# Softmax attention in a two-layer decoder trunk: weights normalised by GpSimd and streamed against values held in column halves

## The chip, the cores and the metric

One core of a Trainium2 chip runs the whole program. The metric is device time in microseconds (us). Engines are called by the letters of the profile: PE (TensorE, the matmul array), PEld (its weight loads), DVE (VectorE), ACT (ScalarE), POOL (GpSimd), SP (SyncE, which issues the weight loads from HBM).

## The reference

Two layers, each a half-weighted SwiGLU FFN, a token mixing and a second such FFN, then a final RMS norm; 256 tokens, width 1024, all in float32. The mixing projects the normalised tokens once (`w_in`) and splits the result over three groups that share the output projection: six retention heads of 64, six attention heads of 64, and a 31-tap causal depthwise convolution over 256 channels. The attention is MoBA, but 256 tokens are a single block of its 256, so it comes down to causal softmax attention over all keys:

```python
s_own = jnp.einsum('bhqd,bhkd->bhqk', qblk, k_own).astype(jnp.float32) * scale
causal = (own * bs + klocal)[None, :] <= qpos[:, None]
s_list = [jnp.where(causal, s_own, -jnp.inf)]
...
p = jax.nn.softmax(jnp.concatenate(s_list, -1), axis=-1).astype(v.dtype)
out = jnp.einsum('bhqk,bhkd->bhqd', p[..., :bs], v_own)
```

## The kernel before

Every large product is a loop over weights that stream from HBM. A weight piece (`raw`) is cut into two parts of reduced precision, `whi` by ACT (L147) and `wlo` by DVE (L148), and each product is three matmuls, L203 to L205. After a piece has been used the loop calls `tick()`. The small work of the mixing (attention, retention, convolution, rotation) is written as generators, the chains: a chain issues some instructions, then says `yield n` to wait n ticks (or until a named mark is done), so its PE instructions stand between the projection's pieces. The order of PE's instructions is the order of the program; on DVE, ACT and POOL a scheduler puts the instructions in an order at build time, and each engine then works through its list in that order.

The attention chain `moba(t)` handles 128 queries (t is 0 or 1). It spawns a `moba_group` for a few heads at a time: three pairs of heads for t = 0, which sees 128 keys, and two pairs, then one, for t = 1, which sees 256. Of each pair the even head goes to one half-group (j = 0) and the odd one to the other (j = 1). In a group, PE writes the mask and the scores to two PSUM banks (L725, L729); DVE takes the maximum of each row (L733); ACT takes the exponentials into the SBUF tile `pr` and the row sums into `sums` (L740). After four ticks PE transposes the weights (L747), ACT copies them to SBUF (L749, `hf`), and PE multiplies them with the values (L759): the weights, 128 x 128, are loaded as the stationary operand and the 64 columns of one head's values are streamed. The result in the bank `po` has queries as partitions. When all groups are through, DVE takes the reciprocal of the sums (L771) and multiplies `po` by it on its way to SBUF (L773); `into_mix` transposes the three 128-column blocks on PE (L781) and `split` cuts them in two parts (ACT L198, DVE L199) into `mT`, the input of the output projection.

Other work that the prediction speaks of: the convolution's taps, 62 instructions on DVE in each layer (L866: two tensors in SBUF, `u` and the running sum `ac`); the rotation of the retention's queries and keys, of which DVE makes two products from PSUM (L699, L700) and POOL the sum of two SBUF tiles of 128 x 384 (L701), four times in each layer; the retention's scores on PE (L794), multiplied by the decay on DVE (L801), which frees the scores' PSUM banks for the next group, and then multiplied with the values (L809); and POOL's multiplications by a broadcast factor in the norm of the retention (L827, 384 columns) and of the convolution (L888, 512 columns), whose factors POOL makes as powers (L476, and L495 elsewhere).

Of the kernel before, what the change touches and what calls it, by code (L numbers as in the profile page):

```python
# [11 lines left out]
F32 = mybir.dt.float32  # L12
# [3 lines left out]
AF = mybir.ActivationFunctionType  # L16
OP = mybir.AluOpType
# [5 lines left out]
P = 128  # L23
# [5 lines left out]
H = 6  # L29
HD = 64  # L30
HW = H * HD
# [24 lines left out]
class Kernel:  # L56
# [166 lines left out]
    def setup(self):  # L223
        nc, c, a = self.nc, self.const, self.a
        self.mhalf = c.tile([P, 8], F32, tag="mhalf", name="mhalf")
        nc.gpsimd.memset(self.mhalf, -0.5)
        warm = c.tile([P, 8], F32, tag="warm", name="warm")
        nc.scalar.activation(warm, self.mhalf, AF.Silu)
        self.x = [c.tile([P, D], F32, tag=f"x{t}", name=f"x{t}") for t in range(NT)]
        for t in range(NT):  # L230
            for h in range(2):
                n = slice(h * 512, (h + 1) * 512)
                nc.sync.dma_start(self.x[t][:, n], a["x"][t][:, n])
        self.row = self.act.tile([P, D + 8], F32, tag="g", bufs=1, name="row")[0:1, :D]
        nc.scalar.dma_start(self.row, a["fgain"][0:1])
        self.ident = self.load("ident", (P, P), eng=nc.scalar)
# [419 lines left out]
    def mix(self, l, cur, nxt):  # L656
        nc, a = self.nc, self.a
        hT = cur.hT
        mT = self.new_hT()
        with self.tc.tile_pool(name=f"mix{l}", bufs=1) as mp:  # L660

            def tl(tag, shape, bufs=1):
                return mp.tile(shape, F32, tag=tag, bufs=bufs, name=self.name(tag))

            def chunk(w, t, free):
                ps = self.mmb()
                self.projA(ps, t, hT, w, HW, free)
                return ps[:, :HW]

            def heads(x):  # L670
                return x.rearrange("p (h d) -> p h d", h=H)
# [34 lines left out]
            def values(tag, ps):  # L706
                v = tl(tag, [P, HW], 2)
                nc.scalar.activation(v, ps, AF.Copy)
                return v

            def groups(t):
                return [(0, 3)] if t == 0 else [(0, 2), (4, 1)]

            def hs(x, h, lo, hi):
                b = (h % 2) * HD
                return x[b:b + HD, h // 2, lo:hi]

            def moba_group(t, g0, nh, po, sums):
                nk = t + 1
                n = nk * P  # L720
                nb = nh * nk
                banks = [self.acc()[:, :nb * P].rearrange("p (h k) -> p h k", h=nh) for _ in range(2)]
                mask = self.mask16[:, 2 * P - n:][:, None, :].to_broadcast([P, nh, n])
                for sc in banks:
                    nc.tensor.matmul(sc, self.ident16, mask, start=True, stop=False)  # L725
                for i in range(nh):
                    for j, sc in enumerate(banks):
                        h = g0 + 2 * i + j
                        nc.tensor.matmul(sc[:, i], hs(mqT, h, t * P, (t + 1) * P), hs(mkT, h, 0, n), start=False, stop=i == nh - 1)  # L729
                nms, prs = [], []  # L730
                for sc in banks:
                    nm = self.small.tile([P, 4], F32, tag="nm", name=self.name("nm"))
                    nc.vector.tensor_reduce(nm[:, :nh], sc, axis=AX.X, op=OP.max, negate=True)  # L733
                    nms.append(nm)
                for j, sc in enumerate(banks):
                    pr = self.scratch()
                    pv = pr[:, :nb * P].rearrange("p (h k) -> p h k", h=nh)
                    for i in range(nh):
                        h = g0 + 2 * i + j
                        nc.scalar.activation(pv[:, i], sc[:, i], AF.Exp, bias=nms[j][:, i:i + 1], accum_out=sums[:, h:h + 1])  # L740
                    prs.append(pr)
                yield 4
                sts = []
                for j in range(2):
                    pt = self.trb()
                    for i in range(nb):
                        nc.tensor.transpose(pt[:, i * P:(i + 1) * P], prs[j][:, i * P:(i + 1) * P], self.ident)  # L747
                    st = self.scratch()
                    nc.scalar.activation(st[:, :nb * P], pt[:, :nb * P], AF.Copy)  # L749
                    sts.append(st)  # L750
                    yield 1
                yield 1
                for j in range(2):
                    for i in range(nh):
                        h = g0 + 2 * i + j
                        for kb in range(nk):
                            c = (i * nk + kb) * P
                            hd = slice(h * HD, (h + 1) * HD)
                            nc.tensor.matmul(po[:, hd], sts[j][:, c:c + P], mv[kb][:, hd], start=kb == 0, stop=kb == nk - 1)  # L759
                self.done.add(f"mg{t}{g0}{l}")  # L760

            def moba(t):
                yield self.has(*[f"{x}{i}{l}" for x in ("mq", "mk") for i in range(t + 1)])
                po = self.acc()
                sums = self.small.tile([P, 8], F32, tag="sm", name=self.name("sm"))
                for h0, nh in groups(t):
                    self.spawn(moba_group(t, h0, nh, po, sums))
                    yield 2
                yield self.has(*[f"mg{t}{h0}{l}" for h0, _ in groups(t)])
                rc = self.small.tile([P, 8], F32, tag="rc", name=self.name("rc"))  # L770
                nc.vector.reciprocal(rc[:, :H], sums[:, :H])  # L771
                yn = tl("w", [P, HW], 5)
                nc.vector.tensor_tensor(heads(yn), heads(po[:, :HW]), rc[:, :H, None].to_broadcast([P, H, HD]), op=OP.mult)  # L773
                yield 2
                into_mix(yn, 3, t)
                self.done.add(f"moba{t}{l}")

            def into_mix(yn, k0, t):
                ps = self.trb()
                for j in range(3):  # L780
                    nc.tensor.transpose(ps[:, j * P:(j + 1) * P], yn[:, j * P:(j + 1) * P], self.ident)  # L781
                sl = (slice(None), slice(k0, k0 + 3), slice(t * P, (t + 1) * P))
                self.split(mT[0][sl], mT[1][sl], ps[:, :HW].rearrange("p (k s) -> p k s", k=3))
# [135 lines left out]
            w = self.take(4)  # L919
            mv = [values("mv", chunk(w, 0, False))]  # L920
            self.spawn(moba(0))
            mv.append(values("mv", chunk(w, 1, True)))
            self.spawn(moba(1))
            w = self.take(4)
            for t in range(NT):
                self.spawn(rot(chunk(w, t, t == 1), t, rqT, "rq"))
            w = self.take(4)
            for t in range(NT):
                self.spawn(rot(chunk(w, t, t == 1), t, rkT, "rk"))
            w = self.take(4)  # L930
            rv = [values("rv", chunk(w, t, t == 1)) for t in range(NT)]
            w = self.take(4)
# [203 lines left out]
```

## Time and profile before

| what | value |
|---|---|
| median of 3 runs | 991.15 us (990.84 to 991.24) |
| profiled execution | 988.81 us |
| its span | 987.0 us |
| mean granted TensorE clock | 0.998 |
| busy: PE, DVE, ACT, POOL | 976.8, 683.8, 537.1, 67.5 us |

The span is the stretch from the first to the last recorded instruction of the profiled execution; the execution's own time lies 1.8 us above it and 2.3 us below the median. Busy shares are averages: PE is busy 99% of the span and DVE 69%, but in the mixing DVE is far busier than on average. One layer takes 485 us, and the second repeats the first's mixing; rows are shown from the first.

### The profile page before, as it was taken

How to read it: one execution, taken by the hardware profiler on the slowest of the kernel's cores; microseconds unless marked ns; L12 is line 12 of the kernel's file. 1: busy time of each engine (PE TensorE's matmuls, PEld its weight loads, DVE VectorE, ACT ScalarE, POOL GpSimd, SP SyncE). 2: the span in 40 equal slices, each digit the busy share in tenths (PEclk: the TensorE clock that was granted, in tenths of full speed). 3: DMA queues.
4: the chain of work that ended last, by engine and by line, in shares of the span. 5: the costliest groups of instructions: out<-in, count | busy, mean ns of one | idle time of the engine just before them, and what ended most of it. 6: DMA issues, size and time to landing. Idle time of an engine off the chain costs nothing.

```text
span 987.0 us, 13779 instructions
## 1 busy us (share of the span) xinstructions
PE 976.8 (99%) x5321; PEld 850.1 (86%) x5321; DVE 683.8 (69%) x1030; ACT 537.1 (54%) x904; POOL 67.5 (7%) x115
## 2 busy tenths in 40 slices
PE   9999999999999999999999999999999999999997
PEld 6888888898998888888888888888989888888885
DVE  5987565669976866666676656566799677666653
ACT  5755555366554755555465555554665456555542
POOL 0101000021140000000000000002100400000000
PEclk9999999999999999999999999999999999999999
DMA  7975555345542855555546464543545346555511
GB/s 258 334 273 178 205 180 180 119 152 190 171 171 70 309 199 174 208 175 206 176 183 223 171 210 173 205 142 136 193 144 199 135 151 254 176 208 173 209 45 43
DMA packets 28580, 180.17 MB, mean 183 GB/s; under 512 B 3425, under 2 KB 3809, under 8 KB 10338
## 3 DMA queue, kind: packets, MB, share of 16 engines
q1 hardware_dynamic: 27216, 175.54, 51.1%
q10 hardware_dynamic: 1298, 3.74, 1.0%
q8 instruction: 42, 0.69, 0.3%
q14 instruction: 24, 0.20, 0.1%
HBM read 178.22 MB, written 1.05 MB: 182 GB/s over the span
## 4 chain that ended last, share of the span: by engine, by line
PE 92%; DVE 5%; ACT 1%; DMA 1%; issue 1%; POOL 0%; SPq 0%; POOLq 0%; ACTq 0%; DVEq 0%
PE mm L209 15%; PE tr L209 15%; PE acc L614 8%; PE acc L613 8%; PE acc L617 8%; PE tr L210 8%; PE mm L210 8%; PE mm L203 4%; PE mm L205 4%; PE mm L204 4%; DVE wlo L148 2%; DVE ac L866 2%; PE acc L209 1%; PE mm L326 1%; PE tr L505 1%; PE acc L809 1%
## 5 line engine op out<-in xcount | busy, mean ns | idle before, releaser
L148 DVE TENSOR_TENSOR wlo<-raw,whi 128x1024 fp32r<-128x1024 f32 (+1 forms) x340 | 397.9, 1181 | 172.8 <-ACT whi L147 168.9
L147 ACT ACTIVATE whi<-raw 128x1024 fp32r<-128x1024 f32 (+1 forms) x340 | 344.0, 1023 | 213.1 <-PE acc L617 84.7
L209 PE MATMUL mm<-hT,whi 128*128 128x512 f32 x640 | 226.1, 391 | 0.0
L209 PE MATMUL tr<-hT,whi 128*128 128x512 f32 x640 | 225.9, 391 | 0.0
L210 PE MATMUL tr<-hT,wlo 128*128 128x256 f32 x640 | 180.5, 282 | 0.0
L210 PE MATMUL mm<-hT,wlo 128*128 128x256 f32 x640 | 180.4, 282 | 0.0
L209 PEld LDWEIGHTS mm<-hT,whi 128*128 128x128 f32 x640 | 120.1, 188 | 25.9
L209 PEld LDWEIGHTS tr<-hT,whi 128*128 128x128 f32 x640 | 120.1, 188 | 25.1
L613 PE MATMUL acc<-whi,hf 128*128 128x512 f32 x352 | 137.7, 391 | 0.0
L614 PE MATMUL acc<-wlo,hf 128*128 128x512 f32 x352 | 137.2, 390 | 0.0
L210 PEld LDWEIGHTS mm<-hT,wlo 128*128 128x128 f32 x640 | 120.8, 189 | 1.4
L210 PEld LDWEIGHTS tr<-hT,wlo 128*128 128x128 f32 x640 | 121.0, 189 | 0.0
L617 PE MATMUL acc<-whi,hf 128*128 128x512 f32 x352 | 113.6, 389 | 0.0
L203 PE MATMUL mm<-whi,hT 128*128 128x384 f32 (+1 forms) x272 | 99.3, 365 | 0.0
L205 PE MATMUL mm<-whi,hT 128*128 128x384 f32 (+1 forms) x272 | 94.2, 346 | 0.0
L204 PE MATMUL mm<-wlo,hT 128*128 128x384 f32 (+1 forms) x272 | 94.1, 346 | 0.0
L617 PEld LDWEIGHTS acc<-whi,hf 128*128 128x128 f32 x352 | 66.1, 188 | 13.9
L599 ACT ACTIVATE s<-part 128x256 f32<-128x256 f32 x80 | 33.2, 416 | 82.2 <-DVE part L215 82.0
L613 PEld LDWEIGHTS acc<-whi,hf 128*128 128x128 f32 x352 | 66.1, 188 | 13.6
L614 PEld LDWEIGHTS acc<-wlo,hf 128*128 128x128 f32 x352 | 66.2, 188 | 12.3
L215 DVE TENSOR_TENSOR part<-part,tr 128x256 f32<-128x256 f32 x80 | 33.5, 419 | 47.3 <-ACT part L214 47.3
L866 DVE SCALAR_TENSOR_TENSOR ac<-u,vec,ac 128x256 f32<-128x256 f32 x120 | 56.6, 525 | 0.0
(179 smaller groups left out, 983.2 us busy)
## 6 DMA issues: line engine op xcount, KB each, us to landing
raw<-in_wgb SPq DMA_DIRECT2D x80, 1024.0 KB, 4.9
raw<-in_wd SPq DMA_DIRECT2D x44, 1024.0 KB, 4.9
raw<-in_win SPq DMA_DIRECT2D x28, 768.0 KB, 5.1
raw<-in_wout SPq DMA_DIRECT2D x8, 1024.0 KB, 4.9
raw<-in_wga SPq DMA_DIRECT2D x6, 1024.0 KB, 5.4
raw<-in_wcv SPq DMA_DIRECT2D x4, 1024.0 KB, 5.0
raw<-in_wga SPq DMA_DIRECT2D x8, 256.0 KB, 5.6
g<-in_fgain ACTq DMA_DIRECT2D x3, 512.0 KB, 3.9
```

Source lines behind the costliest of these rows:

```text
L147: nc.scalar.activation(hi[:, c], src, AF.Copy)
L148: nc.vector.tensor_tensor(lo[:, c], src, hi[:, c].bitcast(F32), op=OP.subtract)
L203: mm(out, ah, wh, start=start, stop=False)
L204: mm(out, ah, wl, start=False, stop=False)
L205: mm(out, al, wh, start=False, stop=stop)
L209: mm(out, wh, x, start=start, stop=False)
L210: mm(out[:, :S], wl, x[:, 0], start=False, stop=stop)
L215: self.nc.vector.tensor_tensor(v, lo, ps[:, :S], op=OP.add)
L613: mm(ys[t][h], hi[:, ts], wh[:, n], start=first, stop=False)
L614: mm(ys[t][h], hi[:, ts], wl[:, n], start=False, stop=False)
L617: mm(ys[t][h], lo[:, ts], wh[:, n], start=False, stop=last)
L866: nc.vector.scalar_tensor_tensor(ac[ct], us, wj, ac[ct], op0=OP.mult, op1=OP.add)
```

## The change

The row sums are kept in two tiles, one for each half-group. Behind each half-group's exponentials POOL now raises its sums to the power -1 (L745 in the new numbering, against a constant tile `mone`) and multiplies the half-group's weights in place by the result, broadcast along the keys (L746). The wait before the transposes of the weights grows from four ticks to six. In the product with the values the operands are exchanged: a head's values, 128 keys x 64 columns, are the stationary operand, the transposed weights are streamed, and even and odd heads are written by turns to the lower and the upper 64 partitions of `po`, which so holds the result transposed. The reciprocal, the normalising multiplication on DVE and the three transposes behind them are gone, and `split` reads `po`. Lines move by 2 above the attention chain, by 6 in its middle (L747 is now L753, L749 is L755, L759 is L766) and by 3 below it.

```diff
--- before.py
+++ after.py
@@ -224,6 +224,8 @@
         nc, c, a = self.nc, self.const, self.a
         self.mhalf = c.tile([P, 8], F32, tag="mhalf", name="mhalf")
         nc.gpsimd.memset(self.mhalf, -0.5)
+        self.mone = c.tile([P, 64], F32, tag="mone", name="mone")
+        nc.gpsimd.memset(self.mone, -1.0)
         warm = c.tile([P, 8], F32, tag="warm", name="warm")
         nc.scalar.activation(warm, self.mhalf, AF.Silu)
         self.x = [c.tile([P, D], F32, tag=f"x{t}", name=f"x{t}") for t in range(NT)]
@@ -737,9 +739,13 @@
                     pv = pr[:, :nb * P].rearrange("p (h k) -> p h k", h=nh)
                     for i in range(nh):
                         h = g0 + 2 * i + j
-                        nc.scalar.activation(pv[:, i], sc[:, i], AF.Exp, bias=nms[j][:, i:i + 1], accum_out=sums[:, h:h + 1])
+                        nc.scalar.activation(pv[:, i], sc[:, i], AF.Exp, bias=nms[j][:, i:i + 1], accum_out=sums[j][:, h // 2:h // 2 + 1])
+                    r = self.small.tile([P, 4], F32, tag="rc", name=self.name("rc"))
+                    g = g0 // 2
+                    nc.gpsimd.tensor_tensor(r[:, :nh], sums[j][:, g:g + nh], self.mone[:, :nh], op=OP.pow)
+                    nc.gpsimd.tensor_tensor(pv, pv, r[:, :nh, None].to_broadcast([P, nh, n]), op=OP.mult)
                     prs.append(pr)
-                yield 4
+                yield 6
                 sts = []
                 for j in range(2):
                     pt = self.trb()
@@ -750,29 +756,26 @@
                     sts.append(st)
                     yield 1
                 yield 1
-                for j in range(2):
-                    for i in range(nh):
-                        h = g0 + 2 * i + j
-                        for kb in range(nk):
-                            c = (i * nk + kb) * P
-                            hd = slice(h * HD, (h + 1) * HD)
-                            nc.tensor.matmul(po[:, hd], sts[j][:, c:c + P], mv[kb][:, hd], start=kb == 0, stop=kb == nk - 1)
+                for i in range(nh):
+                    pair = g0 // 2 + i
+                    for kb in range(nk):
+                        c = (i * nk + kb) * P
+                        for j in range(2):
+                            hd = slice(pair * P + j * HD, pair * P + (j + 1) * HD)
+                            o = po[j * HD:(j + 1) * HD, pair * P:(pair + 1) * P]
+                            nc.tensor.matmul(o, mv[kb][:, hd], sts[j][:, c:c + P], start=kb == 0, stop=kb == nk - 1)
                 self.done.add(f"mg{t}{g0}{l}")
 
             def moba(t):
                 yield self.has(*[f"{x}{i}{l}" for x in ("mq", "mk") for i in range(t + 1)])
                 po = self.acc()
-                sums = self.small.tile([P, 8], F32, tag="sm", name=self.name("sm"))
+                sums = [self.small.tile([P, 4], F32, tag=f"sm{j}", name=self.name("sm")) for j in range(2)]
                 for h0, nh in groups(t):
                     self.spawn(moba_group(t, h0, nh, po, sums))
                     yield 2
                 yield self.has(*[f"mg{t}{h0}{l}" for h0, _ in groups(t)])
-                rc = self.small.tile([P, 8], F32, tag="rc", name=self.name("rc"))
-                nc.vector.reciprocal(rc[:, :H], sums[:, :H])
-                yn = tl("w", [P, HW], 5)
-                nc.vector.tensor_tensor(heads(yn), heads(po[:, :HW]), rc[:, :H, None].to_broadcast([P, H, HD]), op=OP.mult)
-                yield 2
-                into_mix(yn, 3, t)
+                sl = (slice(None), slice(3, 6), slice(t * P, (t + 1) * P))
+                self.split(mT[0][sl], mT[1][sl], po[:, :HW].rearrange("p (k s) -> p k s", k=3))
                 self.done.add(f"moba{t}{l}")
 
             def into_mix(yn, k0, t):
```

The program's order on three engines, each at one place in the first layer's mixing.

POOL, from the end of the rotation of the attention's keys (`w_2370`) to that of the retention (`w_2583` and on), before:

```order
L687 TENSOR_TENSOR r_513_2372<-w_2370,pc 128x96
L688 TENSOR_TENSOR r_514_2373<-w_2370,pn 128x96
L689 TENSOR_TENSOR w_2370<-r_513_2372,r_514_2373 128x6x16
L701 TENSOR_TENSOR w_2583<-w_2583,w_2584 128x384
L701 TENSOR_TENSOR w_2683<-w_2683,w_2684 128x384
L701 TENSOR_TENSOR w_2734<-w_2734,w_2735 128x384
```

The same place now, from the first half-group's weights (`hf_2453`, t = 0; their power stands just ahead) on; the `sm` tiles hold sums and the `rc` tiles their inverses:

```order
L746 TENSOR_TENSOR hf_2453<-hf_2453,rc_2457 128x384
L745 TENSOR_TENSOR rc_2464<-sm_2438,mone 128x3
L746 TENSOR_TENSOR hf_2460<-hf_2460,rc_2464 128x384
L745 TENSOR_TENSOR rc_2534<-sm_2517,mone 128x2
L746 TENSOR_TENSOR hf_2531<-hf_2531,rc_2534 128x512
L745 TENSOR_TENSOR rc_2540<-sm_2518,mone 128x2
L746 TENSOR_TENSOR hf_2537<-hf_2537,rc_2540 128x512
L745 TENSOR_TENSOR rc_2577<-sm_2517,mone 128x1
L746 TENSOR_TENSOR hf_2575<-hf_2575,rc_2577 128x256
L745 TENSOR_TENSOR rc_2582<-sm_2518,mone 128x1
L746 TENSOR_TENSOR hf_2580<-hf_2580,rc_2582 128x256
L703 TENSOR_TENSOR w_2599<-w_2599,w_2600 128x384
```

With that power twelve instructions have come between the two, and all of them stand ahead of the retention's first sum (now L703).

ACT, where the last weights of t = 1 are made, before (`hf_2545` is the second half of t = 0's transposed weights, `hf_2565` and `hf_2567` are t = 1's last weights):

```order
L708 ACTIVATE mv_2496<-mm_2419 128x384
L749 ACTIVATE hf_2511<-tr_2507 128x384
L740 ACTIVATE hf_2527,sm_2514<-acc_2515,nm_2523 128x256 x2
L740 ACTIVATE hf_2530,sm_2514<-acc_2516,nm_2525 128x256 x2
L749 ACTIVATE hf_2545<-tr_2541 128x384
L740 ACTIVATE hf_2565,sm_2514<-acc_2555,nm_2561 128x256
L740 ACTIVATE hf_2567,sm_2514<-acc_2556,nm_2563 128x256
L147 ACTIVATE whi_2597<-raw_2426 128x768
```

And now, where t = 0's second half is `hf_2597`, and t = 1's last weights are `hf_2575` and `hf_2580`:

```order
L710 ACTIVATE mv_2505<-mm_2421 128x384
L742 ACTIVATE hf_2531,sm_2517<-acc_2519,nm_2527 128x256 x2
L742 ACTIVATE hf_2537,sm_2518<-acc_2520,nm_2529 128x256 x2
L755 ACTIVATE hf_2563<-tr_2559 128x384
L742 ACTIVATE hf_2575,sm_2517<-acc_2565,nm_2571 128x256
L742 ACTIVATE hf_2580,sm_2518<-acc_2566,nm_2573 128x256
L755 ACTIVATE hf_2597<-tr_2593 128x384
L147 ACTIVATE whi_2613<-raw_2428 128x768
```

The copy of t = 0's second half has moved behind t = 1's last exponentials.

DVE, around the retention's decays, before (`hf_2904` and `hf_2906` are t = 0's, `hf_2919` and `hf_2921` t = 1's first):

```order
L866 SCALAR_TENSOR_TENSOR ac_436_2027<-u_2025,vec,ac_436_2027 128x256
L866 SCALAR_TENSOR_TENSOR ac_437_2028<-u_2025,vec,ac_437_2028 128x256
L148 TENSOR_TENSOR wlo_2846<-raw_2746,whi_2845 128x1024
L148 TENSOR_TENSOR wlo_2856<-raw_2746,whi_2855 128x1024
L148 TENSOR_TENSOR wlo_2873<-raw_2783,whi_2872 128x1024
L148 TENSOR_TENSOR wlo_2883<-raw_2783,whi_2882 128x1024
L801 TENSOR_TENSOR hf_2904<-acc_2896,decay 128x384
L801 TENSOR_TENSOR hf_2906<-acc_2897,decay 128x384
L866 SCALAR_TENSOR_TENSOR ac_436_2027<-u_2025,vec,ac_436_2027 128x256
L866 SCALAR_TENSOR_TENSOR ac_437_2028<-u_2025,vec,ac_437_2028 128x256
L801 TENSOR_TENSOR hf_2919<-acc_2909,decay 128x512
L801 TENSOR_TENSOR hf_2921<-acc_2910,decay 128x512
```

And now, where the decays are L804 and the taps L869:

```order
L869 SCALAR_TENSOR_TENSOR ac_436_2029<-u_2027,vec,ac_436_2029 128x256
L148 TENSOR_TENSOR wlo_2852<-raw_2756,whi_2851 128x1024
L148 TENSOR_TENSOR wlo_2862<-raw_2756,whi_2861 128x1024
L869 SCALAR_TENSOR_TENSOR ac_437_2030<-u_2027,vec,ac_437_2030 128x256
L148 TENSOR_TENSOR wlo_2879<-raw_2789,whi_2878 128x1024
L148 TENSOR_TENSOR wlo_2889<-raw_2789,whi_2888 128x1024
L804 TENSOR_TENSOR hf_2910<-acc_2902,decay 128x384
L804 TENSOR_TENSOR hf_2912<-acc_2903,decay 128x384
L869 SCALAR_TENSOR_TENSOR ac_436_2029<-u_2027,vec,ac_436_2029 128x256
L804 TENSOR_TENSOR hf_2925<-acc_2915,decay 128x512
L804 TENSOR_TENSOR hf_2927<-acc_2916,decay 128x512
```

Four instructions of DVE are gone from each layer, but the first decay is only two places nearer to the start of its list (the 332nd instead of the 334th): two more taps stand ahead of it.

## Rows read from the trace of the kernel before

**Rows 1.** The page: each engine's busy time in us, share of the span, instructions

```profile
PE 976.8 (99%) x5321; PEld 850.1 (86%) x5321; DVE 683.8 (69%) x1030; ACT 537.1 (54%) x904; POOL 67.5 (7%) x115
```

**Rows 2.** Windows in the mixing: stretch, length, each engine's busy time (instructions), clock, DMA

```profile
245.00:260.00 15.00, 15.00 (x104) 14.85 (x104) 14.94 (x29) 6.83 (x12) 2.87 (x3) 1.00 0.43 145
260.00:275.00 15.00, 15.00 (x108) 14.53 (x107) 15.00 (x23) 10.79 (x14) 1.48 (x2) 1.00 0.47 149
```

**Rows 3.** Waits of PE's weight loads, 225 to 300 us: total, times, longest

```profile
PEld acc L759 <- ACT hf L749: 0.5, 1, 0.5
...
PEld acc L794 <- DVE hf L801: 0.2, 1, 0.2
```

**Rows 4.** DVE's timeline around the decays: start, time from first to last end

```profile
275.65 1.00 DVE L801 TENSOR_TENSOR hf<-acc,decay 128x384 f32<-128x384 f32 x2
276.59 0.86 DVE L866 SCALAR_TENSOR_TENSOR ac<-u,vec,ac 128x256 f32<-128x256 f32 x2
277.37 1.27 DVE L801 TENSOR_TENSOR hf<-acc,decay 128x512 f32<-128x512 f32 x2
```

**Rows 5.** PE's timeline at the same place, the projection's rows left out

```profile
272.82 1.83 PE L794 MATMUL acc<-rqT,rkT 64*128 64x128 f32 x28
...
276.86 0.72 PE L794 MATMUL acc<-rqT,rkT 64*128 64x128 f32 x8
278.66 1.67 PE L809 MATMUL acc<-rv,hf 128*128 128x64 f32 x14
```

**Rows 6.** DVE's timeline where the attention's result is normalised

```profile
245.34 0.54 DVE L773 TENSOR_TENSOR w<-acc,rc 128x384 f32<-128x384 f32 x1
245.81 0.17 DVE L771 RECIPROCAL rc<-sm 128x6 f32<-128x6 f32 x1
245.91 1.68 DVE L866 SCALAR_TENSOR_TENSOR ac<-u,vec,ac 128x256 f32<-128x256 f32 x3
```

**Rows 7.** POOL's timeline, 220 to 300 us

```profile
253.79 1.12 POOL L701 TENSOR_TENSOR w<-w,w 128x384 f32<-128x384 f32 x1 [7.28 <-DVE w L700]
...
285.50 1.36 POOL L476 TENSOR_TENSOR rstd<-ms,mhalf 128x6 f32<-128x6 f32 x1
286.94 0.83 POOL L827 TENSOR_TENSOR w<-rg,rstd 128x384 f32<-128x384 f32 x1
...
291.60 1.04 POOL L888 TENSOR_TENSOR hf<-hf,rstd 128x512 f32<-128x512 f32 x1
```

**Rows 8.** Taps at 245.8, 253.5 and 266.7 us: shortest/median/longest in ns

```profile
L866 DVE SCALAR_TENSOR_TENSOR ac<-u,vec,ac x3: 472/472/883, 245.9 to 247.1; 128x256 f32<-128x256 f32 x3
L866 DVE SCALAR_TENSOR_TENSOR ac<-u,vec,ac x3: 470/471/1232, 253.6 to 255.1; 128x256 f32<-128x256 f32 x3
L866 DVE SCALAR_TENSOR_TENSOR ac<-u,vec,ac x9: 467/468/1239, 266.8 to 270.7; 128x256 f32<-128x256 f32 x9
```

**Rows 9.** DVE's timeline: weight splits at 263 and 285 us

```profile
263.58 2.35 DVE L148 TENSOR_TENSOR wlo<-raw,whi 128x1024 fp32r<-128x1024 f32 x2
...
285.67 1.22 DVE L148 TENSOR_TENSOR wlo<-raw,whi 128x1024 fp32r<-128x1024 f32 x1 [0.59 <-ACT whi L147]
```

**Rows 10.** POOL's powers of one column, from the whole span: ns

```profile
L495 POOL TENSOR_TENSOR r<-e,mhalf x12: 567/569/580, 191.1 to 982.3; 128x1 f32<-128x1 f32 x12
```

**Rows 11.** PE's timeline in the attention, the projection's rows left out

```profile
242.75 0.88 PE L759 MATMUL acc<-mv,hf 128*128 128x64 f32 x6
...
248.87 0.49 PE L781 MATMUL tr<-ident,w 128*128 128x128 f32 x3
249.20 0.38 PE L747 MATMUL tr<-ident,hf 128*128 128x128 f32 x2
...
250.48 1.89 PE L759 MATMUL acc<-mv,hf 128*128 128x64 f32 x16
```

**Rows 12.** ACT's timeline at the copy of t = 0's second half

```profile
243.49 0.50 ACT L749 ACTIVATE hf<-tr 128x384 f32<-128x384 f32 x1
...
244.67 0.23 ACT L740 ACTIVATION_READ_ACCUMULATOR hf<-acc,nm 128x1 f32 x1
```

## The prediction

> **What bounds the kernel now.** I read the page first. PE is busy 99% of the span and POOL 7% [rows 1], so at first sight only PE counts and POOL has time to give away. The windows correct that for the place of the change: from 245 to 275 us DVE is busy 29.94 of 30 us [rows 2], against 69% over the whole span. In the mixing PE and DVE are both full, and the question is which of them the other waits for.
>
> The waits of PE's weight loads answer it [rows 3]. There are two that name an engine. One, 0.5 us, is the product with the values waiting for ACT's copy of the transposed weights. The other, 0.2 us, is the retention's scores (L794) waiting for DVE's decays (L801), which free the scores' banks. The timelines show this second place closely: DVE's first decays run from 275.65 to 276.65 [rows 4], and PE's next eight score matmuls start at 276.86 [rows 5]; DVE's second decays run from 277.37 to 278.64 [rows 4], and PE's L809, which reads them, starts at 278.66 [rows 5]. So DVE is the gate here, with nothing to spare, and PE arrives almost at the same moment. DVE has had no idle time for some 30 us before, so whatever makes DVE later in the attention arrives undiminished at this gate. Whatever makes PE earlier is waited away there.
>
> **What the change takes from DVE.** In each layer two L773 and two L771 go. From start to start these take 0.47 and 0.10 us (245.34, 245.81, 245.91) [rows 6], together 1.14 us. But the order of DVE shows two more taps ahead of the first decay; a tap in this place takes 0.39 us (276.59 to 277.37 for two) [rows 4]. At the gate DVE is therefore only 1.14 - 0.78 = 0.36 us earlier in each layer.
>
> **What it changes on PE.** The three transposes of L781 take 0.33 us (248.87 to 249.20) [rows 11], twice in a layer: 0.66 us gone. A pass of 128 columns there takes 0.33/3 = 0.11 us. The product with the values has 18 matmuls in each layer and, in fp32, two passes for each: 36 records before (6 of them at 242.75, 16 at 250.48 in 1.89 us, or 0.118 us each [rows 11]) and 36 now, but each now streams 128 columns instead of 64. One after the other they would take 36 x 0.11 = 4.0 us against some 36 x 0.118 = 4.2. If the two column halves run side by side, as the two row halves of L794 seem to do (28 matmuls of 128 columns in 1.83 us [rows 5], 0.065 each), they take 36 x 0.065 = 2.3 us. PE so wins 0.8 to 2.5 us in each layer. At the gate none of it counts. It won't even reach it: ACT's copy of t = 0's second half ended at 243.9 [rows 12] and now stands behind t = 1's last exponentials, which end at 244.9 [rows 12] and which will be later themselves, since their maxima wait on DVE. With the two added ticks (twelve projection matmuls; PE runs 104 instructions in 15.00 us [rows 2], so some 12 x 0.144 = 1.7 us) PE comes to its product at 242.75 + 1.7 = 244.5 [rows 11], and waits there for an estimated 2 us. I take no change from PE, and no change from this wait: both lie in front of a gate at which PE waits longer.
>
> **What it adds on POOL.** Twelve instructions in each layer. POOL's multiplications by a broadcast factor take 0.83 us for 384 columns and 1.04 for 512 [rows 7]; by the line through both, 256 columns take 0.62. Two of each: 2 x (0.83 + 1.04 + 0.62) = 5.0 us. A power takes 0.57 us for one column [rows 10] and 1.36 for six [rows 7], so about 0.73 for two and 0.89 for three; two of each, 4.4 us. POOL has nothing else to do here until the retention's sum L701, which now waits behind all twelve: of them 2 x (0.73 + 1.04 + 0.57 + 0.62) = 5.9 us are t = 1's, so that POOL is through near 251 if it starts on them at 244.9 [rows 12] or before; and the rotated tile is first needed on PE behind t = 1's product, which ends after 252 [rows 11]. As POOL's own work this is hidden.
>
> **What POOL's work does to DVE.** This is the term that decides. A tap takes 0.47 us. In each of the stretches in which POOL has an L701 under way, one tap takes much longer: 0.88, 1.23 and 1.24 us [rows 8], and the fourth L701 repeats the last. The excess is 0.41, 0.76, 0.77 and 0.77 us, 0.68 on average. A POOL operation of the same 384 columns that isn't itself waiting takes 0.83 us [rows 7], so DVE stood still for 0.68/0.83 = 81% of POOL's work; L701's longer 1.12 us [rows 7] is then its own wait for the tap under way. The taps and weight splits, which fill DVE's list wherever the new multiplications fall, have both inputs in SBUF; L746 reads SBUF as L701 does. With the same share the multiplications cost DVE 0.81 x 5.0 = 4.0 us in each layer.
>
> The powers are another matter. The one at 285.50 ran for 1.36 us [rows 7], and the weight split that DVE started inside it, at 285.67, took 1.22 us, as much as the splits at 263.58, two in 2.35 us, with POOL idle [rows 9]. So a power doesn't hold DVE, and I cost it at nothing; if it held it as a multiplication does, it would cost 0.81 x 4.4 = 3.6 us in each layer.
>
> The Trainium skill (SBUF — State Buffer, section Who interferes with whom) says that a DVE instruction with two SBUF inputs contends with a GpSimd instruction that reads SBUF, and that whoever comes first holds the shared pair of ports for its whole instruction. By this the multiplications would cost up to their full length, and so would the powers, which read SBUF too. The trace agrees for L701 to 81% and speaks against it for the power; I go by the trace.
>
> **The sum.** In each layer +4.0 (multiplications) - 0.36 (DVE's own savings at the gate) + 0 (powers, PE, ACT) = +3.7 us, and both layers are alike: +7.4 us. On the profiled execution that is 988.81 + 7.4 = 996.2; the median of the runs lies 2.34 us above it, so **998.6 us** on its scale. The bounds of the unknown: with the least of the four excesses, 0.41/0.83 = 49%, the multiplications cost 2.5 us and the sum is 2 x 2.1 = 4.2 us, 995.4; with their whole length it is 2 x 4.64 = 9.3 us, 1000.4.
>
> **The rivals.**
>
> *The powers hold DVE as well.* Each layer then loses 4.0 + 3.6 - 0.36 = 7.2 us, and the time is 991.15 + 14.5 = 1005.6. For it speaks that a power reads two SBUF tiles as a multiplication does; against it stands the split at 285.67. It would need POOL's power to block in many short reads that the one row doesn't show.
>
> *Part of the delay is hidden.* The multiplications fall partly beside DVE instructions that read PSUM (the maxima, L773's neighbours L699 and L700), or the half-groups at the end fall in a stretch in which PE is late anyway, so that about half of the 4.0 us counts: 2 x (2.0 - 0.36) = 3.3, 994.4. Against it: of DVE's time in this stretch most is taps and splits.
>
> *Nothing is held.* If L746 doesn't collide with DVE (its broadcast factor is tiny, and its one large tile might be read in another way than L701's two), the gate stays where it is, DVE is 0.36 us earlier, and PE's savings are waited away: 991.15 - 0.7 = 990.4, no change. L701's four collisions speak against it.
>
> *PE's gain comes through.* This ends on the other side. If the multiplications cost DVE nothing and the wait at the decays isn't the limit that I take it for (the 0.2 us could be the last of several conditions, and DVE's list could be shortened by what PE frees earlier), PE's 2.2 us (0.66 of transposes and, between its bounds, some 1.5 of the product) count in each layer: 991.15 - 4.4 = 986.8. It decides only where DVE reaches its first decays at least 2 us earlier than now, and the order gives it 0.36.
>
> **How the numbers follow.** A measurement of this kernel tells from no change what is more than about 0.2%, or 2.0 us. I give the forecast 0.60, the powers' rival 0.10, the hidden part 0.12, no collision 0.11 and PE's gain 0.07. Slower by over 0.2% are the first three, 0.82; the same is the fourth, 0.11; faster the last, 0.07. The forecast's own range is 995.4 to 1000.4. The range leaves out the last two cases and takes in the others with a little room: 993 to 1006.
>
> **What would show it.** In the profile of the changed kernel the taps and splits of DVE in the attention should show maxima of 1.1 to 1.5 us, six of them in each layer, each inside an L746, and those beside an L745 alone their usual 0.47. PE should wait for L804 for 3 to 4 us in each layer where it waited 0.2, and for L755 for 1 to 2 us at the first product with the values. The decays should start near 279.3 instead of 275.65. L766 should take 0.07 to 0.11 us for each pass. The granted clock should stay at its upper level; should PE's waits of 3 to 4 us bring the lower one, of which no row here tells the price, the time would be above my range. The prediction is wrong if the decays start near 275 and PE still waits, or if L746 takes far longer than 1.04 us for 512 columns.

## The result, and the profile after

The changed kernel takes 995.99 us (median of 10 runs, 991.46 to 1000.06) where the kernel before takes 990.73 in the same comparison: ratio 1.0053, 95% interval 1.0039 to 1.0068, or 5.3 us slower. The forecast was slower by 7.4. The runs lie far apart, in step with the granted clock: 991.46 us at 0.998 and 1000.06 at 0.992. The profiled execution has 994.32 us, a span of 992.5 and a clock of 0.995.

The page, first the busy times, answers to [rows 1]: POOL has gained 33.5 us, DVE 1.6 us with eight instructions fewer.

```profile
PE 976.6 (98%) x5309; PEld 846.1 (85%) x5309; DVE 685.4 (69%) x1022; ACT 537.9 (54%) x904; POOL 101.0 (10%) x140
```

The windows of the mixing (columns as in [rows 2]) show a loss that the prediction did not have: from 230 to 245 us PE is busy for 12.46 us, DVE for 13.11, against 14.59 and 15.00 before, and the granted clock is 0.91. The last row, a narrower window, is at 0.50, the lower of the clock's two levels (1.2 GHz); the whole stretch at that level goes from 242.4 to 245.8, and the second layer has one as long.

```profile
230.00:245.00 15.00, 12.46 (x73) 9.46 (x71) 13.11 (x27) 9.37 (x28) 9.79 (x5) 0.91 0.45 154
245.00:260.00 15.00, 15.00 (x110) 13.59 (x111) 15.00 (x27) 7.64 (x16) 9.36 (x9) 0.97 0.42 143
...
242.60:245.30 2.70, 2.70 (x10) 1.58 (x11) 0.81 (x4) 1.20 (x5) 2.54 (x4) 0.50 0.69 255
```

POOL's timeline gives the start of it:

```profile
234.98 6.49 POOL L745 TENSOR_TENSOR rc<-sm,mone 128x3 f32<-128x3 f32 x1 [8.19 <-ACT hf L742]
241.54 0.82 POOL L746 TENSOR_TENSOR hf<-hf,rc 128x384 f32<-128x384 f32 x1
242.33 1.03 POOL L745 TENSOR_TENSOR rc<-sm,mone 128x3 f32<-128x3 f32 x1
```

The first power takes 6.49 us; the next, of the same size, 1.03. DVE's timeline at that time:

```profile
234.10 4.03 DVE L869 SCALAR_TENSOR_TENSOR ac<-u,vec,ac 128x256 f32<-128x256 f32 x10
238.06 2.68 DVE L148 TENSOR_TENSOR wlo<-raw,whi 128x768 fp32r<-128x768 f32 x3
240.66 1.27 DVE L735 TENSOR_REDUCE nm<-acc 128x2 f32<-128x512 f32 x2
241.86 1.18 DVE L869 SCALAR_TENSOR_TENSOR ac<-u,vec,ac 128x256 f32<-128x256 f32 x2
244.94 0.75 DVE L735 TENSOR_REDUCE nm<-acc 128x1 f32<-128x256 f32 x2 [1.89 <-PE acc L731]
...
278.35 1.01 DVE L804 TENSOR_TENSOR hf<-acc,decay 128x384 f32<-128x384 f32 x2
```

Ten taps and three weight splits follow one another at full speed, all with two inputs in SBUF, and the power ends 0.8 us after the first instruction that reads PSUM (the maxima at 240.66). It was not POOL that held DVE but DVE that held POOL. PE's timeline shows what waited (the projection's rows left out):

```profile
242.42 0.90 PE L753 MATMUL tr<-ident,hf 128*128 128x128 f32 x3 [2.54 <-POOL hf L746]
...
243.68 1.23 PE L731 MATMUL acc<-mkT,mqT 64*128 64x256 f32 x4
...
255.26 1.09 PE L766 MATMUL acc<-hf,mv 128*64 128x128 f32 x16
256.28 0.44 PE L753 MATMUL tr<-ident,hf 128*128 128x128 f32 x2
...
275.43 1.83 PE L797 MATMUL acc<-rqT,rkT 64*128 64x128 f32 x28
279.48 0.71 PE L797 MATMUL acc<-rqT,rkT 64*128 64x128 f32 x8
```

PE idles 2.54 us at the first transposes, then runs at the lower clock, the next scores (L731) take 1.23 us and come late, and DVE waits 1.89 us for them. The chain that ended last now goes through POOL here:

```profile
234.98 6.50 POOL rc L745
241.54 0.83 POOL hf L746
242.42 0.90 PE tr L753 x3
243.75 1.21 PE acc L731 x4
245.69 1.02 DVE ac L869 x2
```

To compare kernels I measure in each layer from the first maxima of t = 0 to two points: PE's first retention scores and DVE's first decays. Before, the maxima start at

```profile
233.41 1.01 DVE L733 TENSOR_REDUCE nm<-acc 128x3 f32<-128x384 f32 x2
```

so PE's scores (272.82 [rows 5]) come 39.41 us later and the decays (275.65 [rows 4]) 42.24. Now the maxima start at 233.17, and it is 42.26 and 45.18: PE is 2.85 us later, DVE 2.94. The second layer repeats both shifts within 0.02. Twice 2.85 is 5.7 us, the result within 0.5. DVE's 2.94 add up as 1.89 (the wait) + 1.21 (four longer instructions beside the multiplications: taps of 0.79, 0.71 and 0.70 us, a split of 1.36) + 0.19 (the rotation's sums, whose excess is 2.90 instead of 2.71) - 0.36 (saved).

How DVE's delay becomes PE's can be read further up, some 9 us ahead of the decays. The projection's matmuls need the bank from which DVE makes the last two products of the rotation. The last product on DVE and the matmul behind it on PE, before (the same matmul, counted back from the scores) and now:

```profile
266.31 0.54 DVE L700 TENSOR_TENSOR w<-mm,rs 128x384 f32<-128x384 f32 x1
267.18 0.34 PE L203 MATMUL mm<-whi,hT 128*128 128x384 f32 x1
...
269.02 0.54 DVE L702 TENSOR_TENSOR w<-mm,rs 128x384 f32<-128x384 f32 x1
269.70 0.41 PE L203 MATMUL mm<-whi,hT 128*128 128x384 f32 x1 [0.72 <-DVE w L702]
```

Before, PE came to this matmul without a wait, 0.33 us behind the product's end at 266.85; now it waits 0.72 us and starts 0.14 behind the end at 269.56. So the two engines met here within 0.2 us before the change. DVE's product ends 2.95 us later than before (36.39 us behind the maxima instead of 33.44), PE's scores start 2.85 later: what PE lost itself, at the transposes and by the clock, counts only as far as DVE had to wait for it (1.89 us), and DVE's delay counts nearly in full.

### The profile page after: what moved, and what is told of

Read it like the earlier page. It is cut to its first block, busy times and chain, and to the rows that moved or that the text cites. A ratio compares the mean times of both kernels' runs of the same rounds, so it can differ in the third digit from the quotient of the medians.

```text
span 992.5 us, 13780 instructions
## 1 busy us (share of the span) xinstructions
PE 976.6 (98%) x5309; PEld 846.1 (85%) x5309; DVE 685.4 (69%) x1022; ACT 537.9 (54%) x904; POOL 101.0 (10%) x140
## 4 chain that ended last, share of the span: by engine, by line
PE 87%; DVE 8%; POOL 2%; issue 1%; DMA 1%; ACT 1%; SPq 0%; POOLq 0%; ACTq 0%; DVEq 0%
PE mm L209 15%; PE tr L209 15%; PE acc L616 8%; PE acc L615 8%; PE acc L619 8%; PE tr L210 8%; PE mm L210 8%; DVE ac L869 3%; DVE wlo L148 3%; PE mm L203 3%; PE mm L205 3%; PE mm L204 3%; PE acc L209 1%; POOL rc L745 1%; PE mm L328 1%
## 5 line engine op out<-in xcount | busy, mean ns | idle before, releaser
L203 PE MATMUL mm<-whi,hT 128*128 128x384 f32 (+1 forms) x272 | 100.0, 367 | 1.4 <-DVE w L702 1.4
L494 POOL TENSOR_SCALAR e<-ss 128x1 f32<-128x1 f32 x12 | 3.2, 268 | 666.6 <-ACT sq L491 666.6
L215 DVE TENSOR_TENSOR part<-part,tr 128x256 f32<-128x256 f32 x80 | 33.5, 419 | 47.3 <-ACT part L214 47.3
```

Of the source, the lines that this page charges most:

```text
L203: mm(out, ah, wh, start=start, stop=False)
L215: self.nc.vector.tensor_tensor(v, lo, ps[:, :S], op=OP.add)
```

## The experiments

The last columns are the shift of the two points in the first and the second layer, in us. PE's, ACT's and DVE's lists are those of the kernel before in e7 and e8 and those of the changed kernel in e9 and e10. In all the others instructions of DVE are added or moved, and in e2, e5, e6 and e12 of ACT as well.

| kernel | median us | ratio to before (95%) | PE's scores | DVE's decays |
|---|---|---|---|---|
| changed kernel | 995.99 | 1.0053 (1.0039 to 1.0068) | +2.85, +2.86 | +2.94, +2.92 |
| e8 before, powers added | 990.74 | 1.0000 (0.9991 to 1.0008) | +0.08, +0.01 | +0.16, +0.10 |
| e7 before, multiplications added | 995.75 | 1.0052 (1.0038 to 1.0067) | +2.11, +1.96 | +2.20, +2.05 |
| e10 small products for powers | 994.37 | 1.0037 (1.0025 to 1.0049) | +1.85, +1.71 | +1.94, +1.78 |
| e11 one-input instruction added | 998.75 | 1.0084 (1.0070 to 1.0098) | +4.16, +5.26 | +2.73, +3.82 |
| e1 inverses on DVE | 996.20 | 1.0056 (1.0043 to 1.0068) | +3.28, +3.25 | +1.85, +1.82 |
| e2 ten ticks | 1000.98 | 1.0091 (1.0075 to 1.0108) | +4.79, +5.42 | +4.46, +4.78 |
| e4 filler on PE | 1001.01 | 1.0110 (1.0094 to 1.0125) | +4.62, +6.01 | +3.92, +4.57 |
| e5 multiplied by ACT | 1008.77 | 1.0185 (1.0172 to 1.0198) | +8.88, +9.21 | +8.51, +8.81 |
| e6 nothing on POOL | 990.59 | 0.9993 (0.9984 to 1.0002) | -0.39, -0.38 | -0.32, -0.33 |
| e9 no normalisation | 990.00 | 0.9996 (0.9988 to 1.0005) | -0.36, -0.35 | -0.29, -0.29 |
| e13 before, rotation's sums on DVE | 990.80 | 1.0000 (0.9992 to 1.0009) | -0.01, -0.02 | -1.45, -1.46 |
| e12 e6 and e13 together | 989.94 | 0.9999 (0.9989 to 1.0009) | -0.40, -0.40 | -1.68, -1.70 |

**e8: the powers alone.**

```diff
 # before.py, behind each half-group's exponentials
+nc.gpsimd.tensor_tensor(self.dz[:, :nh], sums[:, g0 + j:g0 + j + 2 * nh - 1:2], self.mone[:, :nh], op=OP.pow)
```

> The kernel before, with the six powers of each layer added on POOL behind the exponentials (written to a tile that nobody reads); the lists of PE, DVE and ACT are the same as before. Theory A (DVE's run of taps and splits holds the power, not the power DVE): the first power takes about 6.5 us again, taps and splits keep their 0.47 and 0.94 us, ratio 1.000 (0.999 to 1.001). Rival (powers hold DVE, 3.6 us in each layer): ratio 1.007.

Taps and time are unchanged: powers take nothing from DVE. They are held themselves. The first power and the second, each from a window of the instructions by line (ns, shortest/median/longest):

```profile
L744 POOL TENSOR_TENSOR dz<-sm,mone x1: 3492/3492/3492, 237.2 to 237.2; 128x3 f32<-128x3 f32 x1
...
L744 POOL TENSOR_TENSOR dz<-sm,mone x1: 2977/2977/2977, 240.8 to 240.8; 128x3 f32<-128x3 f32 x1
```

And DVE's timeline:

```profile
239.92 0.17 DVE L775 RECIPROCAL rc<-sm 128x6 f32<-128x6 f32 x1
...
242.99 1.27 DVE L736 TENSOR_REDUCE nm<-acc 128x2 f32<-128x512 f32 x2
```

The first lasted 3.49 us, until 0.8 us behind the start of the reciprocal, the second 2.98, until 0.8 us behind that of the maxima. The old kernel's reciprocal, which has one SBUF input, split the run in two. The change removes it, and so lengthened the run that holds its own power to 6.5 us. But the hold doesn't always come: in the second layer, with the same lists and beside the same nine taps, the first power took 1.11 us, and only the second was held, until 0.8 us behind the start of the reciprocal (2.29 us).

**e7: the multiplications alone.**

```diff
 # before.py, at the same place
+nc.gpsimd.tensor_tensor(self.dz[:, :nb * P].rearrange("p (h k) -> p h k", h=nh), pv, self.mone[:, :nh, None].to_broadcast([P, nh, n]), op=OP.mult)
```

> The kernel before, with the six multiplications of each layer added on POOL behind the exponentials (weights times a broadcast constant, written to a tile that nobody reads); the lists of PE, DVE and ACT are the same as before. It measures what the multiplications alone take from DVE. By the prediction's 81% they take 4.0 us in each layer: decays near 279.6, ratio to before 1.008. By what the changed kernel and the run with DVE's reciprocal showed (taps 0.24 to 0.55 us longer, nothing where DVE reads PSUM), 1.5 to 2.5 us in each layer: ratio 1.003 to 1.005.

They cost DVE 2.1 us in each layer, half of the prediction's 4.0, and the kernel 5.0 us. In the profiled execution the clock is 1.00 through both mixings, and PE's shifts alone make 4.1 us: the loss needs no fall of the clock. PE again waits at L203 for the rotation's last product (0.73 us). And a large instruction can be held as well. The second layer's first multiplication, by line (ns):

```profile
L744 POOL TENSOR_TENSOR dz<-hf,mone x1: 3442/3442/3442, 722.6 to 722.6; 128x384 bf16<-128x384 f32 x1
```

DVE's timeline beside it:

```profile
721.68 3.64 DVE L870 SCALAR_TENSOR_TENSOR ac<-u,vec,ac 128x256 f32<-128x256 f32 x9
725.24 0.18 DVE L775 RECIPROCAL rc<-sm 128x6 f32<-128x6 f32 x1
```

It took 3.44 us, past the reciprocal, while nine taps ran undisturbed. In the first layer the same one took 1.07, and two taps 1.04 each instead of 0.47. Whether POOL gets in between two taps or not until the run breaks is not settled by the program's order alone; what settles it stays open.

**e10: the powers replaced by small multiplications** (the weights are scaled by minus the sums, not by their inverses).

```diff
-nc.gpsimd.tensor_tensor(r[:, :nh], sums[j][:, g:g + nh], self.mone[:, :nh], op=OP.pow)
+nc.gpsimd.tensor_tensor(r[:, :nh], sums[j][:, g:g + nh], self.mone[:, :nh], op=OP.mult)
```

> The changed kernel with POOL's powers replaced by multiplications of the same few sums by the same constant, so that the weights are scaled by minus the sums and not by their inverses; all lists keep their order. Theory A, that it is the power that DVE's run holds: the first small multiplication takes under 1 us, PE doesn't wait at the first transposes, DVE doesn't idle before the third maxima; the weights' multiplications now fall among taps. Ratio to before 1.002 to 1.005, and 0.997 to 1.000 to the changed kernel. Rival, that any POOL instruction behind DVE's run is held: the first one takes 6 us as before, and the time stays at 1.005.

The first small multiplication in POOL's timeline:

```profile
237.13 5.81 POOL L745 TENSOR_TENSOR rc<-sm,mone 128x3 f32<-128x3 f32 x1 [8.19 <-ACT hf L742]
```

The rival was right on the hold: it isn't peculiar to the power as an operation. Theory A's range for the time was met all the same (1.0037), but not for its reason. The shorter instruction spares PE 0.6 us of the wait (1.9 instead of 2.5), and the kernel is 1 us in each layer ahead of the changed one.

**e11: the run broken.**

```diff
+nc.vector.reciprocal(rd[:, :nh], sums[j][:, g:g + nh])
 nc.gpsimd.tensor_tensor(r[:, :nh], sums[j][:, g:g + nh], self.mone[:, :nh], op=OP.pow)
```

> The changed kernel with a DVE reciprocal added behind each half-group's exponentials (its result is read by nobody; POOL's power and multiplication stay). The reciprocal has one SBUF input and stands among the taps, where the reciprocal L771 stood before the change. If a POOL instruction held by DVE's run of two-input instructions gets in at the first one-input instruction, the first power ends with the first reciprocal, after 1 to 3.5 us instead of 6.5, and PE doesn't wait at the first transposes. Rival: it is the power's own length or its wait for ACT, and it takes 6 us again. In time the two nearly agree, since the multiplications then fall among taps: 1.003 to 1.006 to before.

The timelines of POOL, DVE and PE, one after the other:

```profile
236.67 2.29 POOL L747 TENSOR_TENSOR rc<-sm,mone 128x3 f32<-128x3 f32 x1 [8.19 <-ACT hf L742]
```

```profile
238.16 0.17 DVE L746 RECIPROCAL rd<-sm 128x3 f32<-128x3 f32 x1
```

```profile
271.15 0.66 PE L203 MATMUL mm<-whi,hT 128*128 128x384 f32 x1 [3.08 <-DVE w L702]
271.61 0.52 PE L204 MATMUL mm<-wlo,hT 128*128 128x384 f32 x1
271.93 0.52 PE L205 MATMUL mm<-whi,hT 128*128 128x384 f32 x1
272.25 0.52 PE L203 MATMUL mm<-whi,hT 128*128 128x384 f32 x1
```

The power ends 0.8 us behind the reciprocal, as the hold has it, and PE doesn't wait at the transposes. But the kernel is slower than expected. The multiplications now fall among taps and splits, DVE is late, and PE waits 3.08 us at another place: the projection's next matmul (L203) needs the bank that the rotation's products (L702) have still to read. Behind that wait the matmuls start 0.32 us apart, about half the pace of those ahead of it (0.17 us apart). The rotation's last product ends 2.70 us late, PE's scores start 4.16 us late: they come 7.42 us behind that product instead of 5.87 in the changed kernel, so the lower clock behind the wait costs some 1.5 us here.

**e1: inverses on DVE.**

```diff
-nc.gpsimd.tensor_tensor(r[:, :nh], sums[j][:, g:g + nh], self.mone[:, :nh], op=OP.pow)
+nc.vector.reciprocal(r[:, :nh], sums[j][:, g:g + nh])
```

> The inverses of the sums are made by a DVE reciprocal for each half-group instead of POOL's power; the multiplications stay on POOL. Theory A (POOL's first power, held for 5.6 us by DVE's taps and splits, makes PE wait 2.5 us, the clock falls, the scores come late and DVE idles 1.9 us): PE's wait before the first transposes is gone, the granted clock is 0.998 in every run, DVE has no idle time before its decays. The first two multiplications now fall among taps, so that up to 0.7 us each of hold is new: ratio to before 1.001 to 1.005, runs within 2 us of each other instead of 9. Theory B (the loss is the multiplications holding DVE, whoever makes the inverse): ratio 1.005 to 1.008, decays 3 to 4 us later than before.

No wait at the first transposes, and yet no gain: as in e11 PE waits at L203 for L702 (2.2 us), and the clock from 260 to 275 us is 0.89. Theory A was right that DVE gains by it: its last product for the rotation ends 1.8 us late instead of 2.95. But PE waits 2.2 us for it where it waited 0.72, and the lower clock behind that wait adds 1.5 us (scores 7.44 us behind the product, against 5.87). So theory A alone doesn't explain the loss, and theory B's later decays (3 to 4 us) didn't come either (1.85).

**e2: later transposes.**

```diff
-                yield 6
+                yield 10
```

> The wait between the exponentials and the transposes of the weights is ten ticks instead of six; the rest as in the changed kernel. Theory A: the power still takes about 6.5 us, but PE reaches the transposes some 4 us later and no longer waits, the clock stays at 0.998, DVE doesn't idle; what is left is the multiplications' hold of 1.2 us less the 0.36 saved: ratio to before 1.001 to 1.003. Theory B: the hold stays as it is, ratio about 1.005.

PE no longer waits at the transposes, but the rotation's transposes (L678) now stand ahead of t = 1's in its list, while the sum that they read (L703) still stands behind all twelve on POOL. PE waits 5.0 us for it. Both theories missed this.

**e4: PE kept busy.**

```diff
+if t == 0 and j == 0:
+    for _ in range(22):
+        nc.tensor.transpose(pt[:, :P], self.ident, self.ident)
```

> 22 transposes of the identity are put in PE's list ahead of the first transposes of the weights (into the same bank, which the real ones overwrite), so that PE works through the 2.5 us in which it waits for POOL. Theory A, with the clock as the middle link: the granted clock is 0.998, the t = 1 scores take 0.7 us instead of 1.2, DVE idles 0.3 to 0.8 us instead of 1.9 in each layer: ratio to the changed kernel about 0.997, to before 1.002 to 1.003, and the runs lie within 2 us of each other. Rival (the clock doesn't matter, the wait alone does): same as the changed kernel, 1.005, or slower.

The clock is 1.00 up to 260 us, the scores take 0.70 us and DVE doesn't idle. But the scheduler gave DVE another list, with nine taps ahead of t = 1's last maxima instead of two, and PE waits later (2.45 us at L203). So it says nothing clean about the clock's share in the changed kernel. It does give the price of one fall of the clock. In both layers the rotation's last product ends 4.71 us late and PE waits for it equally long:

```profile
271.42 0.42 PE L203 MATMUL mm<-whi,hT 128*128 128x384 f32 x1 [2.45 <-DVE w L702]
...
762.29 0.66 PE L203 MATMUL mm<-whi,hT 128*128 128x384 f32 x1 [2.45 <-DVE w L702]
```

In the first layer the clock stays at 1.00 and PE's scores are 4.62 us late; in the second it is 0.69 from 760 to 765 us and they are 6.01 late, 1.4 us more.

**e5: ACT multiplies, POOL makes the inverses.**

```diff
-nc.gpsimd.tensor_tensor(pv, pv, r[:, :nh, None].to_broadcast([P, nh, n]), op=OP.mult)
+for i in range(nh):
+    nc.scalar.activation(pv[:, i], pv[:, i], AF.Copy, scale=r[:, i:i + 1])
```

> The powers stay on POOL, the weights are multiplied by ACT, one instruction for each head. Theory A: the first power is still held for 6.5 us; ACT, which has the weights' multiplication in its list ahead of weight parts, waits for it, so that PE and DVE wait for weight parts as well: ratio to before 1.003 to 1.010. Theory B (only the multiplications on POOL cost): ratio 1.000.

Theory A's mechanism, at twice its price: ACT stands behind the held power (5.07 us), the weight parts and the copies behind ACT; PE waits 5.8 us for copies, DVE 8.2 for weight parts.

**e6, e9: nothing on POOL.** e6 takes the DVE line of e1 and the ACT lines of e5; e9 removes L745 and L746 altogether (no normalisation).

> Nothing on POOL: the inverses are DVE reciprocals and the weights are normalised by ACT, one instruction of 0.37 to 0.47 us for each head. Theory A and theory B agree that both holds are gone: ratio to before 0.999 to 1.001, since DVE still sets the decays and is only about 0.5 us earlier; if ACT's twelve added instructions (about 5 us in each layer) make the weight parts late, 1.002 or more.

> The changed kernel without any normalisation (no powers, no multiplications; the weights go in as exponentials): it leaves the exchange of operands, the lost transposes and DVE's lost four instructions. If DVE sets the decays, PE's savings are waited away and only DVE's 0.36 us in each layer count: ratio to before 0.999 (0.998 to 1.000). Rival, that PE's 2 us in each layer come through: 0.995 to 0.996.

Without POOL the loss is gone, and the exchange of operands gains nothing that these runs can tell from no change. Since e9 has the changed kernel's lists on PE, ACT and DVE, the 3.2 us between them in each layer (+2.85 and -0.36) are the work of POOL's twelve instructions. In e9 PE waits 1.5 us at L203 for L702, which is where its savings go:

```profile
267.40 0.41 PE L203 MATMUL mm<-whi,hT 128*128 128x384 f32 x1 [1.46 <-DVE w L702]
```

**e13, e12: the rotation's sums on DVE**, in the kernel before and in e6.

```diff
-nc.gpsimd.tensor_tensor(z, z, t2, op=OP.add)
+nc.vector.tensor_tensor(z, z, t2, op=OP.add)
```

> The kernel before with the rotation's four sums in each layer on DVE instead of POOL. By the trace each L701 on POOL takes 0.4 to 0.8 us from DVE's taps; the same sum on DVE should take about 0.4 to 0.5 us from start to start. If POOL's hold is real, DVE is 0.5 to 1.2 us earlier at the decays of each layer and the ratio to before is 0.997 to 0.999; if the longer taps have another cause, DVE is 1.9 us later in each layer: 1.004.

> The exchange of operands with nothing on POOL in the attention and the rotation: inverses by DVE reciprocals, weights normalised by ACT, the rotation's sums on DVE. The version with ACT alone gave 0.9993; with the hold of the four L701 gone as well DVE should be some 0.8 us earlier in each layer: ratio to before 0.996 to 0.999. Rival, that PE is now the bound: as that version, 0.999.

DVE gets to the decays 1.45 us earlier though it does more itself, so POOL's hold is real. But PE's scores don't move and the time doesn't either: DVE being earlier at the decays gains nothing. No version tried is faster than the kernel before.

## Why the prediction was right, and where not

The direction, the culprit (POOL's new work beside a full DVE) and the range held. The sum of 7.4 us against 5.3 is near by luck in part, for two steps failed.

- **"DVE is the gate here"**, at the decays: right on the engine and wrong on the place. In every kernel measured PE's second scores start 4.04 or 4.05 us behind the first, though DVE's decays move against the first scores, from 1.45 us earlier to 0.09 later; and the profile shows 0.2 us of wait there in the changed kernel as before, and in e13 too, where the decays are 1.45 us earlier. The wait of 3 to 4 us that I forecast there did not come. So the wait that I read as the end of a full engine was no lever. Nor are there only two waits that name an engine, as I wrote: the list behind [rows 3] has three more, of 0.2 to 0.3 us. What a DVE over 0.1 us later than now at the decays would cost is not shown, since no kernel has it. PE and DVE meet further up: at L203, which waits for the rotation's last product (L702). Where PE waits there and the clock stays up behind it (the changed kernel, e7, e9, e10), PE's shift follows that of the product within 0.1 us: +2.85 on +2.95, +2.11 on +2.20, -0.36 on -0.28, +1.85 on +1.94. The shift of PE's first scores, doubled, gives every kernel's time within 1.5 us.
- **"As POOL's own work this is hidden"**: wrong, and this is the step that missed the larger part of DVE's delay, the 1.89 us of waiting. I asked only whether POOL holds DVE. DVE held POOL's first power for 5.6 us, PE waited 2.54, and the clock fell.
- **Multiplications, 4.0 us in each layer**: mis-sized. 2.1 with the old lists (e7), 1.2 in the changed kernel, where the held power moved them beside maxima and into DVE's wait.
- **Powers cost DVE nothing**: right (e8, 1.0000). The rival of 1005.6 falls.
- **PE's product at 0.065 us a pass**: right; 16 passes take 1.02 us (255.26 to 256.28), 0.064 each, side by side in the column halves. That the gain would be waited away is right as well (e9), though at L203 and not at the decays.
- **A wait of about 2 us for ACT's second copy**: not there in the changed kernel; PE was late itself.
- **The clock**: forecast to stay up, its fall named as a risk without a price. In the profiled execution it fell in both layers, for 3.4 us each. Of that the 2.5 us up to the end of t = 1's scores (242.42 to 244.91) count, since DVE waits for these. My estimate: at the upper level they take half as long, and DVE's wait and the loss shrink by some 1.2 us in each layer. That is 2.4 of the 5.5 us between the two profiled executions. No run shows it in the changed kernel by itself, since e4 changed DVE's list too. The other executions have clocks from 0.992 to 0.998 and times that follow them, so their share differs.

What each of POOL's two effects is worth cannot be added up: take away the held instruction (e1, e11) and the multiplications fall among taps, and PE waits elsewhere.

## What to carry to other kernels

Before work goes to an idle POOL, look at what DVE runs at that moment: where that is a run of instructions with two SBUF inputs, POOL may have to wait for the whole run, and its consumer with it. Ask of a contended resource who holds whom in both directions. A short wait at the end of a busy stretch is only a gate if the waiting engine moves when the other does: compare the distance between two of its own rows across kernels. Two engines that meet within a few tenths of a us lose in full by either's delay and gain nothing by either's saving alone, as PE and DVE do at L203.

## What the runs showed of the hardware

- A POOL instruction of three columns took 6.49 us (power) and 5.81 us (multiplication) beside an unbroken run of DVE instructions with two SBUF inputs, and 2.29 to 3.49 us where a reciprocal broke the run; in one layer of e8 it took 1.11 us beside the same taps. The Trainium skill (SBUF — State Buffer, section SBUF: two separate sides) says that the first to start gets the shared ports for its whole instruction. These runs go beyond it: ten DVE instructions (seven taps and three splits, between 234.98 and 240.66 us) started one after another ahead of a POOL instruction that was already under way. Read with that rule, DVE got the ports ten times in a row ahead of a waiting POOL; the ports themselves no trace shows.
- After PE's idle time of 2.54 us the granted clock was 0.50 for 3.4 us; after 3.08 us (e11) it was 0.52 from 271 to 274 us; after 1.5 us (e9) it stayed at 1.00. After 2.45 us (e4) it stayed at 1.00 in one layer and fell in the other, so the idle time just before doesn't settle it alone.
- One such fall behind a wait made PE's next scores 1.4 us (e4) to 1.5 us (e1, e11) later.
